# Reversed queries with one 24 KB bias table, and query and gate writes issued by ScalarE, in a hybrid decoder block

## The chip, the cores and the metric

The kernel runs on one core of one Trainium2 chip. The metric is device time in microseconds (us), lower is better; a time given for a kernel is the median of its runs. A profiled execution of the kernel before gives the trace from which all rows here are taken. The engines: TensorE (PE; PEld are its weight loads), VectorE (DVE), ScalarE (ACT), GpSimd (POOL) and SyncE (SP). SP and ACT also issue DMAs; their instruction queues appear as SPq and ACTq.

## The reference, cut to what matters

One decoder block over 512 tokens of width 1024, in float32. A state-space branch (S5) and a sliding-window attention run in parallel on the same normalized input, are merged by gates, projected and added to the input; a mixture of 16384 single-neuron experts (PEER) follows. The part that is changed is attention, with its queries, its relative-position bias and the gates' way to memory:

```python
q = rms_norm(q.reshape(bsz, seq, N_KV_HEADS, Q_PER_KV, HEAD_DIM), q_norm_g)   # 16 heads of 64
scores = jnp.einsum('bnqkgd,bnskd->bnkgqs', qb, kb).astype(jnp.float32) * scale   # blocks of 128 queries, 256 keys
dist = ATTN_BLOCK + qi - si
band_ok = (dist >= 0) & (dist < WINDOW)
bias = rel_bias_table.astype(jnp.float32)[t5_bucket(jnp.maximum(dist, 0))]
scores = jnp.where(valid, scores + bias, NEG_INF)
m = jnp.maximum(jnp.max(scores, axis=-1, keepdims=True), sink)
p = jnp.exp(scores - m)
p = p / (jnp.sum(p, axis=-1, keepdims=True) + jnp.exp(sink - m))
out = jnp.einsum('bnkgqs,bnskd->bnqkgd', p.astype(vb.dtype), vb)
gates = jax.nn.sigmoid(gate_logits + b_gate[layer])
```

The bias of a head depends on the distance of query and key alone. So all of it, for 128 queries and 256 keys, is a table of 384 numbers for each head, read at a shifted place for each query.

## The kernel before, in words

Large products are made to full precision by splitting both sides into a rounded part and a rest (`hi`, `lo`; `split`, L84 to L90) and adding three products (`mm3`, L92 to L96). A weight unit of 128x1024 numbers is loaded by SyncE into `raw` (three buffers, L117), rounded to `hi` by ScalarE (L124) and its rest `lo` made by VectorE, or now and then by GpSimd (L125).

Stages, in order. `front` projects keys and values (`proj_kv`), queries (`proj_q`), the state-space input (`proj_u`) and 16 gate tiles (`proj_gates`). Into the first three is woven `s5_params`, a long chain of small operations on VectorE and GpSimd (powers, rotations `sqr` and `sqi`, tables `co` and `si`, products `kps` on TensorE). `s5_mix` runs beside the first gates. Then attention: `kv_prep`, then for each of 4 blocks of queries `attn_q` (queries are loaded from memory and transposed, `qtr`, L597), for each of 16 units `attn_scores` (L620 products, L621 norm and bias, softmax) and `attn_pv` (probabilities transposed, `ptr`, L645, then the product with the values, `pvo`), with the products of `glu`, `s5_branch` and `attn_branch` as filling. The end of attention lies near 415 us; the PEER stage takes the rest of the time.

How the changed parts work before:

- `proj_q` (L541): for each of 2 halves of the heads and 4 blocks of tokens, ScalarE evacuates the product twice, as `qt` (L549, two buffers under the tag e1) and squared as `sq` (L550); VectorE sums the squares into `ssq` (L551); SyncE writes `qt` to memory, `q_d` (L553), 256 KB each. After the last, VectorE and ScalarE make the reciprocal norms `rq` (L556, L557).
- `proj_gates` (L559): VectorE multiplies (L567), ScalarE takes Tanh (L568), SyncE writes the tile to `g_d` (L569), 256 KB each, 16 times. SyncE executes in order, so weight loads behind such a write are issued after it.
- `bias_table` (L655): one small product gives `rb_m`, 16 heads x 384 numbers. ScalarE's queue writes it 128 times into `bias_d` (L668), 3 MB, so that a load with a step of 383 numbers from partition to partition (L669) finds each query's row shifted by one the other way. The load `bias` (L833), 2 MB, is issued before attention.

The order on each engine is not written by hand in this part: a scheduler sets it from the order of the program and its own estimate of times. So a change of one operation can move others.

Of the kernel before, what the change touches and what calls it, by code (L numbers as in the profile page):

```python
# [10 lines left out]
F32 = mybir.dt.float32  # L11
# [5 lines left out]
ALU = mybir.AluOpType  # L17
# [4 lines left out]
NT = T // 128  # L22
KD = D // 128
EPS = 1e-6
# [3 lines left out]
def r32(ap):  # L28
    return ap.bitcast(F32)
# [29 lines left out]
class Builder:  # L59
# [481 lines left out]
    def proj_q(self, xh, xl, ssq, qd, pool):  # L541
        nc = self.nc
        ep = self.ep
        for g in range(2):
            def ev_q(j, ps, g=g):
                qt = ep.tile([128, 512], F32, tag="e1", name=self.nm("qt"))
                sq = ep.tile([128, 512], F32, tag="e2", name=self.nm("sq"), bufs=1)
                r = self.rx[:, j:j + 1]
                nc.scalar.activation(qt, ps, AF.Copy, scale=r)  # L549
                nc.scalar.activation(sq, ps, AF.Square, scale=r)  # L550
                nc.vector.tensor_reduce(ssq[:, j, 8 * g:8 * g + 8], sq.rearrange("p (h d) -> p h d", d=64),  # L551
                                        axis=AX.X, op=ALU.add)
                nc.sync.dma_start(out=qd[j, :, 512 * g:512 * g + 512], in_=qt)  # L553
            yield from self.proj_tok(xh, xl, 512 + 512 * g, ev_q)
        rms = pool.tile([128, NT * 16], F32, name="rms")
        nc.vector.tensor_scalar(rms, ssq.rearrange("p a b -> p (a b)"), 1.0 / 64, EPS, op0=ALU.mult, op1=ALU.add)  # L556
        self.rq = self.rsqrt(pool, rms, NT * 16).rearrange("p (a b) -> p a b", b=16)  # L557

    def proj_gates(self, xh, xl, bg, gd):  # L559
        nc = self.nc  # L560
        for m in range(16):
            wh, wl = self.unit_cols(self.i["w_in"], 2048 + m * 128, 128)
            ps = self.gpsum[0].tile([128, T], F32, tag=self.gpsum[1], name=self.nm("gps"))
            for k in range(KD):
                self.mm3(ps, wh[:, k, :], wl[:, k, :], xh[:, k, :], xl[:, k, :], k == 0, k == KD - 1)
            g = self.ep.tile([128, T], F32, tag="e1", name=self.nm("gt"))
            nc.vector.tensor_mul(g, ps, self.rb)  # L567
            nc.scalar.activation(g, g, AF.Tanh, bias=bg[:, m:m + 1], scale=0.5)  # L568
            nc.sync.dma_start(out=gd[m], in_=g)  # L569
            yield 5.2  # L570

    def kv_prep(self, kv, kH, kL, vH, vL, gk):
# [15 lines left out]
    def attn_q(self, pool, n, qd, gq):  # L588
        nc = self.nc
        q = pool.tile([128, D], F32, tag="a_q", name=self.nm("a_q"), bufs=1)  # L590
        nc.sync.dma_start(out=q, in_=qd[n])
        qs = pool.tile([128, 16, 128], F32R, tag="a_qs", name=self.nm("a_qs"))
        for g in range(2):
            ps = self.ptr.tile([128, 4, 128], F32, tag="tr", name=self.nm("qtr"))
            for i in range(4):
                c = (4 * g + i) * 128
                nc.tensor.transpose(ps[:, i, :], q[:, c:c + 128], self.ident)  # L597
            for par in range(2):
                src = slice(64 * par, 64 * par + 64)
                oth = slice(64 - 64 * par, 128 - 64 * par)  # L600
                hs = slice(8 * g + par, 8 * g + 8, 2)
                nc.scalar.activation(qs[src, hs, :], ps[src], AF.Copy, scale=gq[src, :])
                nc.vector.scalar_tensor_tensor(qs[oth, hs, :], ps[src], gq[src, :], r32(qs[src, hs, :]),
                                               op0=ALU.mult, op1=ALU.subtract)
        return qs
# [30 lines left out]
    def attn_pv(self, pool, n, kvh, sc, vH, vL, aH, aL, psum):  # L636
        nc = self.nc
        nk = 1 if n == 0 else 2
        fl = lambda a: a.rearrange("p a b -> p (a b)")
        po = psum[0].tile([128, 4, 128], F32, tag=psum[1], name=self.nm("pvo"))  # L640
        half, v = divmod(kvh, 2)
        for kk in range(nk):
            ps = self.ptr.tile([128, 4, 128], F32, tag="tr", name=self.nm("ptr"))
            for i in range(4):
                nc.tensor.transpose(ps[:, i, :], sc[:, i, kk * 128:kk * 128 + 128], self.ident)  # L645
            ph = pool.tile([128, 4, 128], F32R, tag="a_ph", name=self.nm("a_ph"))
            pl = pool.tile([128, 4, 128], F32R, tag="a_pl", name=self.nm("a_pl"))
            self.split(ph, pl, ps)
            kt = n if n == 0 else n - 1 + kk
            vs = slice(128 * half, 128 * half + 128)  # L650
            self.mm3(fl(po), vH[:, kt, vs], vL[:, kt, vs], fl(ph), fl(pl), kk == 0, kk == nk - 1)
        rows = slice(64 * v, 64 * v + 64)
        a = (rows, slice(4 * half, 4 * half + 4), slice(n * 128, n * 128 + 128))
        self.split(aH[a], aL[a], po[rows])

    def bias_table(self, pool, dp):
        nc, I = self.nc, self.i
        tab = pool.tile([32, 16], F32, name="rb_t")
        oh = pool.tile([32, 384], F32, name="rb_o")
        mk = pool.tile([16, 384], F32, name="rb_m")  # L660
        nc.scalar.dma_start(out=tab, in_=I["rel_bias"])
        nc.scalar.dma_start(out=oh, in_=I["bucket_onehot"])
        nc.scalar.dma_start(out=mk, in_=I["band_mask"])
        ps = self.ptr.tile([16, 384], F32, tag="tr", name="rb_p")
        nc.tensor.matmul(ps, tab, oh, start=True, stop=True)
        nc.vector.tensor_add(mk, mk, ps)
        bd = dp.tile([16, 128, 384], F32, name="bias_d")
        nc.scalar.dma_start(out=bd, in_=mk[:, None, :].to_broadcast([16, 128, 384]))  # L668
        return bass.AP(tensor=bd.tensor, offset=bd.offset + 127, ap=[[383, 128], [128 * 384, 16], [1, 256]])  # L669

    def glu(self, pool, yg, zH, zL):
        nc = self.nc
# [729 lines left out]
    def consts(self, pool):  # L1402
        nc = self.nc
        self.ident = pool.tile([128, 128], F32, name="ident")
        make_identity(nc, self.ident)
        first = pool.tile([128, 1], F32, name="first")
        nc.vector.memset(first, 0.0)
        nc.scalar.activation(first, first, AF.Square)
        self.iota16 = pool.tile([128, 128, 8], F16, name="iota16")
        nc.gpsimd.iota(self.iota16, pattern=[[1, 128], [0, 8]], base=0, channel_multiplier=0, allow_small_or_imprecise_dtypes=True)  # L1410
# [67 lines left out]
```

## Time and profile before

| What | Value |
|---|---|
| Median of 3 runs | 1686.6 us (1686.0 to 1687.74) |
| Profiled execution, own time | 1682.35 us |
| Its span in the trace | 1680.6 us |
| TensorE busy | 1612.1 us, 96% of the span |
| VectorE busy | 1423.3 us, 85% |
| ScalarE busy | 840.6 us, 50% |
| GpSimd busy | 528.5 us, 31% |
| Written to memory, read from memory | 56.23 MB, 375.66 MB |

The span is what the profiler sees of the execution; 1.75 us lie around it. The share of busy time is a mean over stages with different limits: a stage's own limit is read from a table of windows, and an engine's gap from the row behind it, which names in brackets how long the engine was idle and what released it.

### The profile page before, as it was taken

To read this page: it belongs to the slowest core of one execution; us is meant where nothing else is said; L and a number is where in the kernel's file an instruction comes from. 1 tells how busy PE (TensorE), PEld (TensorE's weight loads), DVE (VectorE), ACT (ScalarE), POOL (GpSimd) and SP (SyncE) were. 2 spreads that over 40 slices of the span, in tenths; PEclk is the share of its full clock that TensorE was granted. 3 is DMA by queue.
4 is the path that set the end of the run, shared out by engine and by line. 5 is a ranking of instruction groups with operands and counts; after the bars stand their busy time and mean duration, and the time that the engine had idled before them with its cause. 6 is when DMAs were issued, how large, how long until landed. Compare 5 with 4: busy or idle time off the path is not lost.

```text
span 1680.6 us, 25288 instructions
## 1 busy us (share of the span) xinstructions
PE 1612.1 (96%) x8831; PEld 1420.8 (85%) x8831; DVE 1423.3 (85%) x2931; ACT 840.6 (50%) x1290; POOL 528.5 (31%) x472
## 2 busy tenths in 40 slices
PE   7789999998999999999999999999999999999998
PEld 5577887786899999989998999888888888888887
DVE  7699868897798899999998975887787887887885
ACT  5256566565565346665776873333333333333332
POOL 2564022332631422222332323332332332332330
PEclk9899999999999999999999999999999999999999
DMA  7823353645764667877886999999999999999993
GB/s 233 156 91 91 113 185 94 195 139 168 219 188 153 227 245 260 290 276 262 285 287 245 330 332 365 324 324 337 336 355 338 335 347 351 328 342 361 360 309 146
DMA packets 239184, 433.56 MB, mean 258 GB/s; under 512 B 17696, under 2 KB 155984, under 8 KB 235984
## 3 DMA queue, kind: packets, MB, share of 16 engines
q1 hardware_dynamic: 175904, 242.69, 43.1%
q0 software_dynamic: 36864, 134.23, 22.6%
q10 hardware_dynamic: 26288, 55.02, 10.2%
q8 instruction: 69, 1.13, 0.3%
q14 instruction: 59, 0.48, 0.1%
HBM read 375.66 MB, written 56.23 MB: 257 GB/s over the span
## 4 chain that ended last, share of the span: by engine, by line
PE 68%; DVE 11%; issue 3%; ACT 2%; DMA 2%; POOL 0%; SPq 0%; DVEq 0%; ACTq 0%; POOLq 0%
PE po L1162 11%; PE po L1161 11%; PE po L1164 11%; PE pa L94 9%; PE pa L96 9%; PE pa L95 8%; DVE lo L125 3%; PE pg L1092 1%; PE pg L1093 1%; DVE sp_row L1211 1%; DVE t_s L966 1%; DVE t_ix L968 1%; DMA raw<-w_ab 1%; DVE t_ix L972 1%; DMA gl<-g_d 1%
## 5 line engine op out<-in xcount | busy, mean ns | idle before, releaser
L124 ACT CAST hi<-t_raw 128x1024 fp32r<-128x1024 f32 x256 | 269.3, 1052 | 229.4 <-PE pa L95 138.2
L125 DVE TENSOR_TENSOR lo<-t_raw,hi 128x1024 fp32r<-128x1024 f32 x256 | 313.4, 1224 | 78.6 <-ACT hi L124 71.2
L94 PE MATMUL pa<-x2h,hi 128*128 128x384 f32 x1024 | 346.9, 339 | 11.2 <-ACT u_g L1136 11.2
L96 PE MATMUL pa<-x2h,lo 128*128 128x384 f32 x1024 | 347.6, 340 | 1.7 <-DVE lo L125 1.7
L95 PE MATMUL pa<-x2l,hi 128*128 128x384 f32 x1024 | 344.9, 337 | 0.0
L1194 POOL DMA_INDIRECT sp_row<-peer_u,sp_ei x128 | 174.3, 1362 | 385.2 <-DVE sp_row L1211 342.6
L1194 POOL DMA_INDIRECT sp_row<-peer_v,sp_ei x128 | 168.5, 1317 | 394.2 <-DVE sp_acc L1213 365.8
L1162 PE MATMUL po<-lo,v_wh 128*128 128x512 f32 x768 | 266.5, 394 | 0.0
L1161 PE MATMUL po<-hi,v_wh 128*128 128x512 f32 x768 | 242.3, 394 | 0.0
L1164 PE MATMUL po<-hi,v_wl 128*128 128x512 f32 x768 | 241.0, 394 | 0.0
L94 PEld LDWEIGHTS pa<-x2h,hi 128*128 128x128 f32 x1024 | 193.5, 189 | 15.6 <-ACT u_g L1136 13.6
L1151 ACT CAST v_wh<-v_w 128x384 fp32r<-128x384 f32 x128 | 65.6, 513 | 275.0 <-DVE v_w L1150 169.1
L96 PEld LDWEIGHTS pa<-x2h,lo 128*128 128x128 f32 x1024 | 193.5, 189 | 4.3 <-DVE lo L125 3.9
L95 PEld LDWEIGHTS pa<-x2l,hi 128*128 128x128 f32 x1024 | 193.4, 189 | 0.9
L1164 PEld LDWEIGHTS po<-hi,v_wl 128*128 128x128 f32 x768 | 143.7, 187 | 35.6
L1162 PEld LDWEIGHTS po<-lo,v_wh 128*128 128x128 f32 x768 | 143.6, 187 | 34.6
L1161 PEld LDWEIGHTS po<-hi,v_wh 128*128 128x128 f32 x768 | 143.5, 187 | 34.0
L1213 DVE SCALAR_TENSOR_TENSOR sp_acc<-sp_row,sp_a,sp_acc 128x1024 f32<-128x1024 f32 x128 | 163.8, 1280 | 0.3
L1211 DVE SCALAR_TENSOR_TENSOR sp_row<-sp_row,xrow 128x1024 f32<-128x1024 f32 x128 | 156.1, 1219 | 4.5 <-DMA sp_row<-peer_u,sp_ei 4.5
L124 ACT CAST hi<-raw 128x1024 fp32r<-128x1024 f32 x88 | 91.9, 1047 | 88.5 <-PE gps L95 15.5
L125 POOL TENSOR_TENSOR lo<-raw,hi 128x1024 fp32r<-128x1024 f32 x28 | 70.3, 2509 | 116.4 <-ACT hi L124 104.6
L1108 ACT COPY g_one<-g_o 128x1024 f16<-128x1024 f16 x48 | 99.1, 2065 | 6.4 <-ACT u_g L1136 2.4
(455 smaller groups left out, 2977.6 us busy)
## 6 DMA issues: line engine op xcount, KB each, us to landing
t_raw<-peer_uT SPq DMA_DIRECT2D x128, 512.0 KB
t_raw<-peer_v SPq DMA_DIRECT2D x128, 512.0 KB
G_d<-g_st ACTq DMA_DIRECT2D x24, 1024.0 KB
v_g<-G_d SPq DMA_DIRECT2D x64, 384.0 KB
raw<-w_in SPq DMA_DIRECT2D x32, 512.0 KB
A_d<-u_g ACTq DMA_DIRECT2D x78, 192.0 KB
v_a<-A_d SPq DMA_DIRECT2D x78, 192.0 KB
raw<-w_ab SPq DMA_DIRECT2D x64, 128.0 KB
```

The lines of the kernel that those rows point to most:

```text
L94: mm(out, lh, rh, start=first, stop=False)
L95: mm(out, lh, rl, start=False, stop=False)
L96: mm(out, ll, rh, start=False, stop=last)
L124: self.nc.scalar.copy(hi, raw)
L125: (self.nc.gpsimd if pool_lo else self.nc.vector).tensor_sub(lo, raw, r32(hi))
L1108: nc.scalar.copy(one, o1.rearrange("p b t -> p t b"))
L1161: mm(po[j][i], wh[:, c], hi[:, hs[i]], start=first, stop=False)
L1162: mm(po[j][i], wh[:, c], lo[:, hs[i]], start=False, stop=False)
L1164: mm(po[j][i], wl[:, c], hi[:, hs[i]], start=False, stop=last)
L1194: nc.gpsimd.indirect_dma_start(out=got[k], out_offset=None, in_=self.i[n], in_offset=bass.IndirectOffsetOnAxis(ap=ei[:, s:s + 1], axis=0))
L1211: nc.vector.scalar_tensor_tensor(r, r, 1.0, xrow, op0=ALU.mult, op1=ALU.mult, accum_out=av[:, s:s + 1])
L1213: nc.vector.scalar_tensor_tensor(acc, r, av[:, s:s + 1], acc, op0=ALU.mult, op1=ALU.add)
```

## The change

Attention's queries are taken in reversed order within their block. A matrix `flip`, ones on the other diagonal, is built at the start, and the product with it takes the place of the transpose in `attn_q`: it transposes the queries and reverses them. With query 127 in partition 0, each partition's row of the bias table begins one number further on than the one before, so a single copy of the table can be read with a step of one number: `bias_d` has 16x384 numbers, 24 KB, in place of 128 copies. Before the product with the values the probabilities are turned back by the same product (`attn_pv`). The reciprocal norms are reversed once, by a product with `flip` and a copy. Scores, softmax and values are computed as before. Besides, the writes of `q_d` and `g_d` are issued by ScalarE.

```diff
                 nc.scalar.activation(sq, ps, AF.Square, scale=r)
...
-                nc.sync.dma_start(out=qd[j, :, 512 * g:512 * g + 512], in_=qt)
+                nc.scalar.dma_start(out=qd[j, :, 512 * g:512 * g + 512], in_=qt)
             yield from self.proj_tok(xh, xl, 512 + 512 * g, ev_q)
-        rms = pool.tile([128, NT * 16], F32, name="rms")
-        nc.vector.tensor_scalar(rms, ssq.rearrange("p a b -> p (a b)"), 1.0 / 64, EPS, op0=ALU.mult, op1=ALU.add)
-        self.rq = self.rsqrt(pool, rms, NT * 16).rearrange("p (a b) -> p a b", b=16)
+        rms = ssq.rearrange("p a b -> p (a b)")
+        nc.vector.tensor_scalar(rms, rms, 1.0 / 64, EPS, op0=ALU.mult, op1=ALU.add)
+        rq = self.rsqrt(pool, rms, NT * 16)
+        ps = self.ptr.tile([128, NT * 16], F32, tag="tr", name="rq_ps")
+        nc.tensor.matmul(ps, self.flip, rq, start=True, stop=True)
+        nc.scalar.copy(rms, ps)
+        self.rq = ssq
...
-            nc.sync.dma_start(out=gd[m], in_=g)
+            nc.scalar.dma_start(out=gd[m], in_=g)
...
-                nc.tensor.transpose(ps[:, i, :], q[:, c:c + 128], self.ident)
+                nc.tensor.matmul(ps[:, i, :], q[:, c:c + 128], self.flip, start=True, stop=True)
...
-                nc.tensor.transpose(ps[:, i, :], sc[:, i, kk * 128:kk * 128 + 128], self.ident)
+                nc.tensor.matmul(ps[:, i, :], sc[:, i, kk * 128:kk * 128 + 128], self.flip, start=True, stop=True)
...
-        bd = dp.tile([16, 128, 384], F32, name="bias_d")
-        nc.scalar.dma_start(out=bd, in_=mk[:, None, :].to_broadcast([16, 128, 384]))
-        return bass.AP(tensor=bd.tensor, offset=bd.offset + 127, ap=[[383, 128], [128 * 384, 16], [1, 256]])
+        bd = dp.tile([16, 384], F32, name="bias_d")
+        nc.scalar.dma_start(out=bd, in_=mk)
+        return bass.AP(tensor=bd.tensor, offset=bd.offset, ap=[[1, 128], [384, 16], [1, 256]])
...
+        self.flip = pool.tile([128, 128], F32, name="flip")
+        nc.gpsimd.memset(self.flip, 0.0)
+        nc.gpsimd.affine_select(out=self.flip, in_=self.flip, compare_op=ALU.not_equal, fill=1.0, base=-127,
+                                pattern=[[1, 128]], channel_multiplier=1)
```

The change also moves instructions. Three places follow, each as the engine's row stands before and then as it stands now; the numbers behind names only tell buffers apart, and lines of the changed kernel are up to 4 higher.

SyncE's queue during the query projection, before: writes of queries (`q_d`) stand between weight loads (`raw`).

```order
L117 DMA raw_1446<-w_in 128x2x512
L553 DMA q_d<-qt_1106 128x512
L117 DMA raw_1511<-w_in 128x8x128
L553 DMA q_d<-qt_1118 128x512
L553 DMA q_d<-qt_1130 128x512
L117 DMA raw_1560<-w_in 128x8x128
L553 DMA q_d<-qt_1142 128x512
L117 DMA raw_1609<-w_in 128x8x128
```

The same queue now:

```order
L117 DMA raw_1451<-w_in 128x2x512
L117 DMA raw_1518<-w_in 128x8x128
L117 DMA raw_1567<-w_in 128x8x128
L117 DMA raw_1616<-w_in 128x8x128
L117 DMA raw_1665<-w_in 128x8x128
```

The writes are gone from between the loads; the same holds further down for the 16 writes of gates.

ScalarE's row in the same place, before: the bias write is issued some rows ahead; the first three blocks of queries are evacuated as `qt` and `sq`.

```order
L668 DMA bias_d<-rb_m 2048x1x384
L103 ACTIVATE rs_s_698<-k_ss 128x16
L124 CAST hi_1096<-raw_1094 128x1024
L124 CAST hi_1242<-raw_1240 128x1024
L103 ACTIVATE rs_s_468<-m_81_461 128x16
L124 CAST hi_1272<-raw_1270 128x1024
L549 ACTIVATE qt_1106<-tps_708,rx 128x512
L550 ACTIVATE sq_1107<-tps_708,rx 128x512
L549 ACTIVATE qt_1118<-tps_709,rx 128x512
L550 ACTIVATE sq_1119<-tps_709,rx 128x512
L549 ACTIVATE qt_1130<-tps_710,rx 128x512
```

ScalarE's row now:

```order
L672 DMA bias_d<-rb_m 16x384
L103 ACTIVATE rs_s_703<-k_ss 128x16
L124 CAST hi_1101<-raw_1099 128x1024
L124 CAST hi_1247<-raw_1245 128x1024
L103 ACTIVATE rs_s_473<-m_81_466 128x16
L124 CAST hi_1277<-raw_1275 128x1024
L549 ACTIVATE qt_1111<-tps_713,rx 128x512
L550 ACTIVATE sq_1112<-tps_713,rx 128x512
L553 DMA q_d<-qt_1111 128x512
L549 ACTIVATE qt_1123<-tps_714,rx 128x512
L553 DMA q_d<-qt_1123 128x512
L550 ACTIVATE sq_1124<-tps_714,rx 128x512
```

The bias write keeps its place and shrinks; each write of queries stands behind the activation that makes its tile.

TensorE's row where the first probabilities are transposed (`ptr`), with the second block of queries (`qtr`) and score products (`scp`) about them, before:

```order
L645 MATMUL ptr_2792<-ident,a_sc_2331 128x128 x4
L597 MATMUL qtr_2848<-ident,a_q_2845 128x128 x2
L620 MATMUL scp_2392<-kH,a_qs_2312 128x256
L620 MATMUL scp_2392<-kL,a_qs_2312 128x256
L620 MATMUL scp_2399<-kH,a_qs_2312 128x256
L620 MATMUL scp_2399<-kL,a_qs_2312 128x256
L597 MATMUL qtr_2848<-ident,a_q_2845 128x128 x2
```

The same place now:

```order
L649 MATMUL ptr_2799<-flip,a_sc_2338 128x128
L624 MATMUL scp_2399<-kH,a_qs_2319 128x256
L624 MATMUL scp_2399<-kL,a_qs_2319 128x256
L624 MATMUL scp_2406<-kH,a_qs_2319 128x256
L624 MATMUL scp_2406<-kL,a_qs_2319 128x256
L649 MATMUL ptr_2799<-flip,a_sc_2338 128x128 x3
L601 MATMUL qtr_2855<-flip,a_q_2852 128x128 x4
```

The products with `flip` take the transposes' places, one for one, and the scheduler groups them and the products about them anew; such moves run through the whole of attention.

## Rows read from the trace of the kernel before

**Rows 1.** Windows: stretch, length, busy TensorE, weight loads, VectorE, ScalarE, GpSimd; clock; DMA.
```profile
60.00:80.00 20.00, 8.26 (x26) 5.95 (x26) 9.48 (x24) 7.38 (x14) 17.19 (x38) 0.73 0.87 177
80.00:108.00 28.00, 28.00 (x133) 23.16 (x133) 27.27 (x128) 14.46 (x25) 14.41 (x35) 0.95 0.38 113
108.00:134.00 26.00, 17.55 (x88) 14.73 (x87) 25.29 (x64) 15.97 (x33) 19.26 (x28) 0.87 0.16 50
...
150.00:205.00 55.00, 55.00 (x313) 47.76 (x312) 53.21 (x95) 29.13 (x66) 3.14 (x9) 1.00 0.37 110
...
250.00:325.00 75.00, 70.85 (x360) 57.89 (x359) 62.79 (x123) 44.27 (x110) 23.92 (x13) 1.00 0.42 126
325.00:385.00 60.00, 54.72 (x369) 48.38 (x370) 58.34 (x114) 38.45 (x93) 18.52 (x9) 1.00 0.56 164
385.00:415.00 30.00, 25.03 (x109) 17.86 (x107) 19.57 (x27) 14.09 (x27) 5.35 (x3) 0.94 0.58 158
```

**Rows 2.** DMA, 38 to 80 us: queue with packets, MB, share; then an issue.
```profile
q10 hardware_dynamic: 2064, 3.15, 65.7%
...
bias_d<-rb_m ACTq DMA_DIRECT2D x1, 3072.0 KB
```

**Rows 3.** Waits, 50 to 85 us: who for what, total us, times, longest.
```profile
ACT qt L549 <- DMA q_d<-qt: 11.4, 1, 11.4
...
ACT hi L124 <- DMA raw<-w_in: 6.3, 1, 6.3
```

**Rows 4.** Timeline of TensorE: start, length, instruction, idle before and its releaser.
```profile
62.79 0.80 PE L94 MATMUL tps<-hi,xh 128*128 128x512 f32 x1 [3.13 <-ACT sq L550]
...
78.94 1.90 PE L94 MATMUL tps<-hi,xh 128*128 128x512 f32 x3 [8.95 <-ACT hi L124]
```

**Rows 5.** Timeline of VectorE: its two gaps, and one multiply twice.
```profile
61.61 1.23 DVE L125 TENSOR_TENSOR lo<-raw,hi 128x1024 fp32r<-128x1024 f32 x1 [2.88 <-ACT hi L124]
...
67.24 0.54 DVE L283 TENSOR_TENSOR cm<-a1r,bb_im 128x128 f32<-128x128 f32 x1
...
78.92 1.23 DVE L125 TENSOR_TENSOR lo<-raw,hi 128x1024 fp32r<-128x1024 f32 x1 [8.85 <-ACT hi L124]
...
80.64 0.28 DVE L283 TENSOR_TENSOR cm<-a2r,bb_im 128x128 f32<-128x128 f32 x1
```

**Rows 6.** Timeline of GpSimd: its wait for the rotations.
```profile
91.16 0.25 POOL L281 TENSOR_TENSOR cm<-co,sqr 128x16 f32<-128x16 f32 x1 [12.72 <-DVE sqi L336]
```

**Rows 7.** Lines L553 and L569: issues, ns least/median/most, first and last.
```profile
L553 SPq DMA_DIRECT2D q_d<-qt x8: 319/339/4722, 62.2 to 107.4; - x8
...
L569 SPq DMA_DIRECT2D g_d<-gt x16: 320/338/339, 152.6 to 255.4; - x16
```

**Rows 8.** Lines L597 and L645: transposes, ns least/median/most, first and last.
```profile
L597 PE MATMUL qtr<-ident,a_q x32: 270/272/328, 221.0 to 342.3; 128*128 128x128 f32 x32
...
L645 PE MATMUL ptr<-ident,a_sc x112: 270/272/421, 253.1 to 411.2; 128*128 128x128 f32 x112
```

**Rows 9.** Timeline of TensorE: two groups of four transposes, two plain products.
```profile
88.40 0.60 PE L417 MATMUL wtr<-ident,w_re 128*128 128x128 f32 x4
88.84 0.60 PE L417 MATMUL wtr<-ident,w_im 128*128 128x128 f32 x4
...
93.94 0.38 PE L426 MATMUL kps<-f_re,wrep 128*128 128x128 f32 x2
94.16 0.39 PE L426 MATMUL kps<-f_im,wrep 128*128 128x128 f32 x2
```

**Rows 10.** Timelines: the bias load and its first use; a load of one line.
```profile
209.60 0.39 ACTq L833 DMA_DIRECT2D bias<-bias_d  x1
...
229.60 0.60 DVE L621 SCALAR_TENSOR_TENSOR a_sc<-scp,rs_y,bias 128x128 f32<-128x128 f32 x2
...
414.96 0.43 SPq L1255 DMA_DIRECT2D xrow<-g2row  x1
...
419.81 2.42 POOL L125 TENSOR_TENSOR lo<-raw,hi 128x1024 fp32r<-128x1024 f32 x1 [2.46 <-DMA xrow<-g2row]
```

## The prediction

> **What bounds the kernel now.** I read the page's busy line first, then a table of windows, then the waits and the DMA view of the window with the most idle time, and at last single rows for prices. TensorE is busy nearly the whole span (the table above), so the question is where it is not. The change ends with the attention stage (about 415 us); behind that every engine keeps its order but for one copy that trades places, so what the front wins or loses moves the end by as much.
>
> The windows [rows 1] show three kinds of stretch. From 60 to 80 us everything but GpSimd stands still: TensorE 8.26 of 20, VectorE 9.48. From 80 to 205 us VectorE is the pacemaker (27.27 of 28, 25.29 of 26, 53.21 of 55), while TensorE has 8.45 us idle between 108 and 134. From 250 us on, the attention stage, TensorE is nearly full (70.85 of 75); in 325 to 385 VectorE is fuller (58.34 of 60, TensorE 54.72); from 385 to 415 neither is (25.03 and 19.57 of 30), and chains of waits set the pace.
>
> Why the hole at 60 us? Queue 10, ScalarE's, takes 65.7% of all 16 DMA engines between 38 and 80 us to move 3.15 MB [rows 2]; the only large transfer there is the write of `bias_d`. Beside it the evacuation `qt` waits 11.4 us for a write of queries, and the cast `hi` 6.3 us for a weight load [rows 3]. TensorE pays with gaps of 3.13 and 8.95 us [rows 4], VectorE with 2.88 and 8.85 us [rows 5].
>
> **The change part by part.** *The bias write shrinks from 3 MB to 24 KB.* That removes the transfer behind both gaps. Upper bound, if TensorE kept its own pace: 3.13 + 8.95 = 12.1 us of gaps, and the low clock around them. At a mean granted clock of 0.73 the 8.26 us busy in 60 to 80 hold 8.26 x 0.27 = 2.2 us of slowness, the 28 us at 0.95 hold 1.4 us [rows 1]; together 15.7 us. But VectorE stands next in line: it is full on both sides of the hole, so it sets what is won. It was idle 2.88 + 8.85 = 11.7 us. During some 10 us of these GpSimd was computing (17.19 of 20 us in the window) [rows 1], and VectorE is slower beside GpSimd: the same multiply takes 0.54 us at 67 us, with GpSimd busy, and 0.28 us at 80.6 us, alone [rows 5]. For the block around it I count a factor of about 1.55 (some operations slow, some not), so 10 us beside GpSimd do 6.5 us of work, and 3.5 us of the hole come back. I take 11.7 - 3.5 = **8.2 us won**. Were every operation slowed by 0.54/0.28 = 1.9, 4.8 us would come back and 6.9 us be won. GpSimd itself has room: it waits 12.72 us for VectorE before 91.16 us [rows 6], more than it loses.
>
> *Queries and gates are written by ScalarE.* The 8 + 16 issues take 0.34 us each [rows 7] and now stand in ScalarE's row behind the activation whose result they send, which is ScalarE's own. That is 2.7 us before 110 us, where ScalarE is half idle (14.46 of 28), and 5.4 us between 150 and 255 us, where it is busy 29.13 of 55 [rows 1] and its casts run ahead of TensorE. Queued behind each issue are the next `qt`, `sq` or `hi`; for them TensorE waits only at group changes. I take 0, at worst the 2.7 us on VectorE's and TensorE's path (the gain is then 4.2). For SyncE the queue is cleared: weight loads no longer stand behind a Tanh. Between 150 and 205 us TensorE is busy all 55 us, so nothing is won by that there. Were SyncE's weight loads in truth held by those writes and not by the volume of the bias write, the gain would be the same, since both go.
>
> *The transposes become products.* 32 transposes of queries and 112 of probabilities [rows 8] are now plain fp32 products with `flip`. A transpose of 128x128 costs TensorE 0.44 / 4 = 0.11 us (four from 88.40 to 88.84); a plain fp32 product of that size stands as two records and costs 0.22 us (93.94 to 94.16) [rows 9]. So 144 x 0.113 = **16.3 us** of work is added to TensorE. Of it 8 products fall near 220 us and 60 (44 + 16) in 250 to 325, where TensorE is full: 68 x 0.113 = 7.7 us, paid. 52 (44 + 8) fall in 325 to 385: 5.9 us, beside 5.28 us of TensorE idle under a full VectorE; I take half the idle time as cover, 2.6 us. 24 fall in 385 to 415: 2.7 us; the products stand in the waited-for chain from scores to the value product, so I count them whole. Cost 16.3 - 2.6 = 13.7 us. Far bounds: with all idle time of 250 to 415 us used (4.15 + 5.28 + 4.97 = 14.4) it would be 1.9 us, with none 16.3 us.
>
> The trace tells of two records for each plain fp32 product, hence twice the transpose. The Trainium skill, page "FP8 and Floating Point Precision", section "TensorE Precision Notes", speaks of four passes for true FP32; if that meant four times the 0.11 us, this part would cost 144 x 0.33 = 47.5 us. No row here shows that price; the 128x128 product says otherwise.
>
> *The bias load reads one 24 KB table.* 2 MB as before in pieces of 1 KB, but all from the same few lines of DRAM. It is issued at 209.60 us and first used at 229.60 us [rows 10], 20 us later. The nearest row of a load that reads one short line for all partitions is `xrow`: 512 KB, issued at 414.96, waited for until 419.81 at the latest [rows 10], so at most 4.9 us; four times that is 19.4 us, still in time. Cost 0, upper end 2 us. *The rest:* the reciprocal norms are turned by one product of 64 columns and one small copy, some 0.3 us about 80 us ahead of their use; `flip` is built on an idle GpSimd at the start. 0.
>
> **Sum.** -8.2 + 13.7 = +5.5 us. The profiled execution took 1682.35 us (span 1680.6), so 1687.9 us on its scale. The three runs have their median at 1686.6, which is 4.25 us above it; on that scale 1686.6 + 5.5 = **1692 us**. Measurement tells 0.2%, that is 3.4 us, from no change.
>
> **The rivals.** *Attention has room for the products* (the other side: faster). The order of that stage is made anew with the products in it: probabilities are turned in groups of up to 8 where groups of 4 stood, further from the value products that wait for them. If this uses more than 8.1 us of the 14.4 us idle, the kernel gets faster. With a cost of 16.3 - 12 = 4.3 us: 1686.6 - 8.2 + 4.3 = 1683 us; with all of it used 1680. For it speaks that TensorE waits there in many small pieces; against, that the pieces are waits for ScalarE and VectorE, which do not become shorter. Chance 0.22.
> *The front gives little back:* VectorE and ScalarE in turn are late, gain 4.2, and the products are paid in full: +12.1 us, 1699. For it speaks VectorE at 97% from 80 us on and the new order, which puts more of the state-space chain ahead of some `lo`. Chance 0.15.
> *TensorE sets the front's pace after all:* the whole 15.7 us are won: 1686.6 - 15.7 + 13.7 = 1685, no difference. Against it speaks VectorE's 27.27 of 28. Chance 0.09.
> *The change does not do what it says:* the gaps at 60 and 70 us stay, because SyncE's loads were late for another reason: +13.7 us, 1700. Against it speaks the 65.7%. Chance 0.03. *Four passes:* 1686.6 - 8.2 + 47.5 - 2.6 = 1723 us. Chance 0.01.
>
> **How the numbers follow.** My forecast, 1692, has a chance of 0.50; its own range is 1687 to 1697 (cover in 325 to 385 between none and all, gain 6.9 to 11.7). Of that 0.13 lies within 3.4 us of before. Of the faster rival 0.04 lies within. So: faster 0.18 + 0.02 (from the third rival's edge) = 0.20; same 0.13 + 0.04 + 0.07 = 0.24; slower 0.37 + 0.15 + 0.03 + 0.01 = 0.56. The range reaches from the faster rival's middle, less its half, 1681, to the second rival, 1699.
>
> **What would show each step.** In the trace of after: the gaps at 60 and 70 us gone, and queue 10 nearly silent before 200 us; VectorE without a hole between 58 and 80 us, and the first gate's Tanh 6 to 10 us earlier. The products: 288 records where 144 stood, and 250 to 415 us longer by 11 to 14 us when measured from the first score product to the last value product. ScalarE with 24 more issues and no new wait of TensorE for it. Wrong I would be if TensorE's idle time in attention shrank by 10 us or more, or if the first Tanh came more than 12 us earlier.

## The result, and the profile after

The changed kernel takes 1696.8 us (median of 5 runs, 1696.4 to 1697.5) against 1686.6 us before: 10.2 us more between the medians, 1.0064 times as long over all runs (95% interval 1.0052 to 1.0075). The forecast was +5.5 us. The sign and the range held; the size came out nearly twice as large.

The profiled execution of the kernel before was a quick one (1682.35 us, below all its other runs). A second profile of the same kernel, taken with the experiments, has a span of 1684.5 us and is used where stages are compared below. At the marks of the table below its front agrees with the first within 0.5 us; of the other 4 us some 2 lie in attention and 2 in PEER.

The stretches of [rows 1], after the change (TensorE, weight loads, VectorE, ScalarE, GpSimd, clock, DMA share, GB/s; four of the windows):

```profile
60.00:80.00 20.00, 15.96 (x67) 11.59 (x66) 19.73 (x63) 8.61 (x15) 16.92 (x36) 0.97 0.26 80
80.00:108.00 28.00, 26.03 (x123) 21.56 (x122) 27.27 (x104) 13.48 (x25) 20.19 (x42) 0.90 0.37 113
108.00:134.00 26.00, 19.30 (x88) 15.13 (x88) 24.76 (x58) 17.82 (x39) 22.01 (x34) 0.93 0.14 41
134.00:150.00 16.00, 13.21 (x69) 11.87 (x70) 13.32 (x27) 9.49 (x18) 3.13 (x5) 0.89 0.32 90
```

The hole at 60 us is gone: VectorE is busy 19.73 of 20 us where it was 9.48, and the DMA share fell from 0.87 to 0.26. But TensorE is not full behind it. It has idle time in every stretch from 60 to 150 us and runs below full clock there.

VectorE's timeline at the second gap of [rows 5], after: the cast `lo` that stood behind 8.85 us of idle time follows at once. The multiply `cm<-a2r,bb_im` now runs beside GpSimd and takes 0.48 us, where it took 0.28 alone at 80.64 us [rows 5].

```profile
67.76 1.21 DVE L125 TENSOR_TENSOR lo<-raw,hi 128x1024 fp32r<-128x1024 f32 x1
68.89 0.48 DVE L283 TENSOR_TENSOR cm<-a2r,bb_im 128x128 f32<-128x128 f32 x1
```

TensorE's timeline of the changed kernel, its idle times between 98 and 137 us (those over 1 us):

```profile
98.31 0.49 PE L426 MATMUL kps<-f_re,wrep 128*128 128x128 f32 x2 [1.90 <-DVE tt L432]
...
120.10 1.12 PE L417 MATMUL wtr<-ident,w_re 128*128 128x128 f32 x4 [3.33 <-DVE tt L432]
...
136.79 0.80 PE L426 MATMUL kps<-f_re,wrep 128*128 128x128 f32 x2 [4.36 <-DVE tt L432]
```

The last of them is the one that matters. For 4.36 us TensorE has nothing that its order lets go ahead, and `tt`, an addition of VectorE that frees the bank for `kps`, came late. Before, TensorE waited in this way one group of `kps` earlier (5.18 us in the first profile, 3.55 in the second) and only 0.16 and 0.81 us at this last one.

The products, as tile views of `qtr` and `ptr` (before: [rows 8]): twice the records for the queries, 64 where 32 stood, and 224 where 112.

```profile
L601 PE MATMUL qtr<-flip,a_q x64: 271/275/377, 217.6 to 350.0; 128*128 128x128 f32 x64
...
L649 PE MATMUL ptr<-flip,a_sc x224: 270/275/422, 251.1 to 423.3; 128*128 128x128 f32 x112
```

### The profile page after: what moved, and what is told of

The parts are those of the page before. It is cut to its first block, busy times and chain, and to the rows that moved or that the text cites. A ratio compares the mean times of both kernels' runs of the same rounds, so it can differ in the third digit from the quotient of the medians.

```text
span 1694.9 us, 25568 instructions
## 1 busy us (share of the span) xinstructions
PE 1631.3 (96%) x8977; PEld 1444.2 (85%) x8977; DVE 1427.0 (84%) x2931; ACT 841.6 (50%) x1291; POOL 528.9 (31%) x474
## 4 chain that ended last, share of the span: by engine, by line
PE 74%; DVE 13%; ACT 5%; DMA 4%; issue 3%; SPq 0%; POOL 0%; ACTq 0%; DVEq 0%; POOLq 0%
PE po L1166 11%; PE po L1165 11%; PE po L1168 11%; PE pa L94 9%; PE pa L96 9%; PE pa L95 9%; DVE lo L125 3%; PE gps L95 1%; PE gps L96 1%; PE pg L1096 1%; PE gps L94 1%; ACT hi L124 1%; PE pg L1097 1%; PE ptr L649 1%; DMA raw<-w_ab 1%
## 5 line engine op out<-in xcount | busy, mean ns | idle before, releaser
L1155 ACT CAST v_wh<-v_w 128x384 fp32r<-128x384 f32 x128 | 65.7, 513 | 283.4 <-DVE v_w L1154 190.1
```

## The experiments

In these sets of runs the kernel before has medians of 1686.2 to 1687.0 us. To follow a gain or a loss through the program, three instructions of TensorE serve as marks: the first product `eps` (the state-space chain is done, the front ends), the last `gps` (the last gate; the first queries are turned in this stretch) and the last `pvo` (attention ends). The starts are in us, from the tile views of each kernel's trace. They are those of one profiled execution, whose own time lies up to 2.6 us to either side of the kernel's median (in the first profile of before 4.3 us below it), so the marks of two kernels compare no better than that.

| Kernel | Median | First `eps` | Last `gps` | Last `pvo` | Span |
|---|---|---|---|---|---|
| before (first profile) | 1686.6 | 147.9 | 252.9 | 414.2 | 1680.6 |
| before (second profile) | 1686.9 | 147.4 | 252.7 | 415.9 | 1684.5 |
| gates' writes moved | 1686.9 | 147.4 | 252.7 | 415.7 | 1684.6 |
| every second query write moved | 1685.1 | 148.0 | 253.0 | 416.0 | 1685.2 |
| queries' writes moved | 1691.4 | 151.7 | 257.0 | 421.3 | 1687.6 |
| both writes moved | 1691.4 | 151.8 | 256.9 | 420.0 | 1687.4 |
| the change without moved writes | 1694.9 | 140.8 | 247.3 | 424.1 | 1693.5 |
| **the change** | 1696.8 | 144.3 | 250.9 | 426.1 | 1694.9 |
| the change, transposes back | 1683.8 | 144.2 | 249.2 | 413.7 | 1682.2 |
| the change, 3 MB write back | 1707.9 | 152.5 | 258.9 | 435.3 | 1704.4 |
| 16 copies, loads on SyncE | 1688.5 | 140.5 | 256.6 | 420.0 | 1689.4 |
| 32 copies, loads on ScalarE | 1678.3 | 140.4 | 244.6 | 407.4 | 1674.8 |
| no moved writes, only queries by product | 1688.7 | 140.9 | 247.6 | 416.5 | 1684.4 |

**Both writes moved, nothing else.** Before, with the two lines of the change that name the issuing engine:

```diff
-                nc.sync.dma_start(out=qd[j, :, 512 * g:512 * g + 512], in_=qt)
+                nc.scalar.dma_start(out=qd[j, :, 512 * g:512 * g + 512], in_=qt)
...
-            nc.sync.dma_start(out=gd[m], in_=g)
+            nc.scalar.dma_start(out=gd[m], in_=g)
```

> Before, with only the 24 writes of queries and gates moved from SyncE to ScalarE; the 3 MB bias write and the transposes stay. Theory A (the 3 MB write's volume makes the hole at 60 us, the queue move is worth nothing): 1686 to 1688 us, first `kps` product within 1.5 us of before's 93.9 us, and the gaps at 62 and 79 us still there. Rival B1 (SyncE's loads are held by the writes that stand ahead of them): the hole shrinks, 1682 to 1684 us. Rival B2 (the order that the scheduler makes with the writes on ScalarE is a worse one; TensorE's gap of 4.36 us at 132 us in the changed kernel comes from it): 1689 to 1691 us.

Measured: 1691.4 us, 1.0033 times before (interval 1.0020 to 1.0046). That is nearest rival B2. The gaps of [rows 4] are still there (3.02 us before 62.27, 8.86 before 78.64) and the first `kps` starts at 94.19 us, so rival B1 falls. The first `eps` comes 4.4 us later than in the second profile of before, and from there the difference stays about the same. So this part, which the forecast put at nothing, costs.

**The change without it.** The two lines above given back to SyncE in the changed kernel.

> The changed kernel with the 24 writes given back to SyncE: the reversal and the 24 KB table alone, in before's order of the front. Theory A: 1696 to 1698 us, as the whole change. Rival B1: weight loads are held again, 1699 to 1701 us. Rival B2 (the moved writes' order costs the front 2 to 4 us): 1693 to 1695 us, and the first exponential of attention 2 to 4 us earlier than in the changed kernel (234.1 us).

Measured: 1694.9 us, again B2, and the first `eps` 3.5 us earlier than in the change (140.8 against 144.3). Against before the front is 6.6 us shorter. The first exponential starts at 230.5 us. Of the 3.5 us the median shows 1.9 (1696.8 - 1694.9), because attention takes 176.8 us here from the last `gps` to the last `pvo` and 175.2 in the change.

**Transposes back.** In the changed kernel:

```diff
-                nc.tensor.matmul(ps[:, i, :], q[:, c:c + 128], self.flip, start=True, stop=True)
+                nc.tensor.transpose(ps[:, i, :], q[:, c:c + 128], self.ident)
...
-                nc.tensor.matmul(ps[:, i, :], sc[:, i, kk * 128:kk * 128 + 128], self.flip, start=True, stop=True)
+                nc.tensor.transpose(ps[:, i, :], sc[:, i, kk * 128:kk * 128 + 128], self.ident)
```

> The changed kernel with the 144 products with the reversed matrix made transposes again (queries are then not reversed, so the biases belong to other queries): what the 24 KB table and the moved writes do without the products. Theory A (the products cost what the two traces show between the first and the last of attention, 15 us): 1681 to 1683 us. Rival C (half of it is the new order of attention, not the products themselves): 1688 to 1690 us. The forecast's own price, 13.7 us: 1683 us.

Measured: 1683.8 us, 0.9984 of before (0.9975 to 0.9992). Between the kernels with and without the 144 products lie 1696.8 - 1683.8 = 13.0 us, nearest to the forecast's 13.7. The expectation of 15 was taken against the quick first profile of before. The time that rival C gave did not come, but this run does not exclude what C says: without the products the scheduler gives attention before's order back, on TensorE, VectorE, ScalarE and GpSimd to the last instruction (issues of DMAs aside). The 13.0 us are thus the price of the products and of attention's new order together.

**The 3 MB write back.** In the changed kernel, behind the write of the 24 KB table; no other instruction changes its place on any engine:

```diff
+        big = dp.tile([16, 128, 384], F32, name="big_d")
+        nc.scalar.dma_start(out=big, in_=mk[:, None, :].to_broadcast([16, 128, 384]))
```

> The changed kernel, and beside its 24 KB table the 3 MB write again, right behind it on ScalarE's queue, to a tensor that nobody reads; every engine's order is that of the changed kernel. Theory A (the write's removal is worth what is left of the front's gain at 205 us, 3.5 us): 1700 to 1701 us. Rival D (it is worth the 8.2 us that VectorE wins up to 80 us, and the moved writes and the new order lose the rest): 1704 to 1706 us. Rival E (the hole has another cause): 1697 us.

Measured: 1707.9 us, 11.1 us above the change and above all three expectations; nearest is D. In the trace the first `eps` is 8.2 us later and the last `pvo` 9.2 us; the profiled execution was 1.6 us quicker than this kernel's median, so the trace does not show where the last of the 11.1 us lie. The timeline of TensorE in this kernel has both gaps of [rows 4] again, within 0.2 us of their old sizes and 0.4 us of their old places, and the DMA issue tells how long the write takes (last figure: us from issue to landing):

```profile
62.88 0.50 PE L94 MATMUL tps<-hi,xh 128*128 128x512 f32 x1 [3.31 <-ACT sq L550]
...
79.25 1.90 PE L94 MATMUL tps<-hi,xh 128*128 128x512 f32 x3 [8.87 <-ACT hi L124]
```

```profile
big_d<-rb_m ACTq DMA_DIRECT2D x1, 3072.0 KB, 36.5
```

So the volume of this one write makes the hole. That part of the theory stands.

**Which of the moved writes costs, and why.** Two kernels move one group of writes each, a third moves four of the eight writes of queries (`nc.scalar if j % 2 else nc.sync`). With the gates' writes alone TensorE, VectorE and GpSimd keep before's order to the last instruction. With the queries' writes alone the whole of the front's new order appears. With every second one before's order stays but for one `lo` of VectorE.

> Before, with only the 16 writes of gates moved to ScalarE. TensorE, VectorE and GpSimd keep before's order. Theory A (an issue on ScalarE delays nothing that TensorE waits for): within 1.5 us of before, 1685 to 1688 us. Rival (16 issues of 0.34 us stand in the way of the casts `hi`): up to 5.4 us more, 1691 us.

> Before, with only the 8 writes of queries moved to ScalarE. The order of the front changes exactly as with all 24 moved. Theory A (the new order is what costs: a cast `lo` now stands ahead of the `tt` for which TensorE waits): 1689 to 1692 us, and the first `eps` product 3 to 5 us later than before's 147.9 us. Rival (the issues on ScalarE cost, most of them being those of the gates): within 1.5 us of before.

> Before, with every second write of queries (4 of the 8) moved to ScalarE. With these four the order comes out as before's on TensorE and GpSimd, and on VectorE but for one `lo`. Theory A (the cost of the moved writes is the new order, not the issues): within 1 us of before up to the first `eps` product, 1686 to 1688 us. Rival (the issues on ScalarE, or the queue that they share, cost): half of what all eight cost, 2 us, 1689 us.

Measured: 1686.9 us for the gates (0.9999, 0.9990 to 1.0008), 1691.4 us for the queries (1.0023, 1.0014 to 1.0032), 1685.1 us for every second query write (0.9989, 0.9980 to 0.9998). Theory A holds in all three (the last came out 0.9 us below its range): issues on ScalarE cost nothing that can be measured, neither sixteen nor four; the order that the scheduler makes with all eight costs some 4 us. A kernel with all eight moved and before's order kept was not run, so that the order does it rests on these three runs and on the rows that follow.

How it costs them is seen on VectorE. In the kernel with only the queries' writes moved, `lo` stands between the copies `up` and the last `tt`:

```profile
137.30 4.88 DVE L500 COPY up<-ut 32x128 f32<-32x128 f32 x8
142.21 1.65 DVE L125 TENSOR_TENSOR lo<-raw,hi 128x1024 fp32r<-128x1024 f32 x1
143.89 0.30 DVE L432 TENSOR_TENSOR tt<-kps,di 32x128 f32<-32x128 f32 x1
```

With every second write moved it stands ahead of `up`, as before, and `tt` ends 1.3 us sooner:

```profile
135.55 1.22 DVE L125 TENSOR_TENSOR lo<-raw,hi 128x1024 fp32r<-128x1024 f32 x1
136.80 0.28 DVE L432 TENSOR_TENSOR tt<-kps,di 32x128 f32<-32x128 f32 x1
137.11 4.79 DVE L500 COPY up<-ut 32x128 f32<-32x128 f32 x8
...
142.55 0.30 DVE L432 TENSOR_TENSOR tt<-kps,di 32x128 f32<-32x128 f32 x1 [0.32 <-ACT tt L434]
```

TensorE pays for it three times. Its timeline with the queries' writes moved, around the `kps` that waits for that `tt`:

```profile
144.24 0.51 PE L426 MATMUL kps<-f_re,wrep 128*128 128x128 f32 x2 [4.38 <-DVE tt L432]
144.57 0.61 PE L426 MATMUL kps<-f_im,wrep 128*128 128x128 f32 x2
...
147.39 0.75 PE L95 MATMUL gps<-xl,hi 128*128 128x512 f32 x1
...
151.68 0.50 PE L449 MATMUL eps<-up,el 128*128 128x128 f32 x3
```

The same place in the second profile of before:

```profile
142.29 0.49 PE L426 MATMUL kps<-f_re,wrep 128*128 128x128 f32 x2 [0.81 <-DVE tt L432]
142.61 0.39 PE L426 MATMUL kps<-f_im,wrep 128*128 128x128 f32 x2
...
144.09 0.47 PE L95 MATMUL gps<-xl,hi 128*128 128x512 f32 x1
...
147.39 0.83 PE L449 MATMUL eps<-up,el 128*128 128x128 f32 x6
```

The window of those eight pairs of `kps` records, in the kernel with the queries' writes moved (the last three numbers: granted clock, DMA share, GB/s):

```profile
144.24:147.39 3.15, 3.15 (x16) 3.15 (x17) 2.99 (x10) 2.00 (x5) 0.20 (x1) 0.55 0.57 167
```

`kps` starts 1.95 us later. After 4.38 us without work TensorE runs the eight pairs in 3.15 us instead of 1.80, at a granted clock of 0.55, near the lower of its two levels (1.2 instead of 2.4 GHz); in the second profile of before it is 1.00 there. That is 1.35 us. And only 7 gate products stood ahead of the wait, where before 10 did; 17 instead of 14 stand between `kps` and `eps`, at 0.23 us each, and the first of them still runs at the low clock (0.58 us to the next, for 0.32). So `eps` begins 4.29 instead of 3.30 us after the first of them: 1.0 us. Together 4.3 us, which is the whole delay of the first `eps` (151.68 against 147.39).

**A short write without the reversal.** If the volume is the cause, fewer copies in memory do as well as none. With 16 copies each of eight loads serves 16 partitions; the loads were given to SyncE, which leaves the order of the other engines as before:

```diff
-        bd = dp.tile([16, 128, 384], F32, name="bias_d")
-        nc.scalar.dma_start(out=bd, in_=mk[:, None, :].to_broadcast([16, 128, 384]))
-        return bass.AP(tensor=bd.tensor, offset=bd.offset + 127, ap=[[383, 128], [128 * 384, 16], [1, 256]])
+        bd = dp.tile([16, 16, 384], F32, name="bias_d")
+        nc.scalar.dma_start(out=bd, in_=mk[:, None, :].to_broadcast([16, 16, 384]))
+        return [bass.AP(tensor=bd.tensor, offset=bd.offset + 127 - 16 * g, ap=[[383, 16], [16 * 384, 16], [1, 256]])
+                for g in range(8)]
...
-        nc.scalar.dma_start(out=bias, in_=bias_src)
+        for g, src in enumerate(bias_src):
+            nc.sync.dma_start(out=bias[16 * g:16 * g + 16], in_=src)
```

> Before, with 16 copies of the bias table instead of 128: a write of 384 KB instead of 3 MB, and eight loads of 16 partitions on SyncE's queue in place of one on ScalarE's; TensorE, VectorE and GpSimd keep before's order to the last instruction. It prices the volume of the write alone. Theory A (worth what the products' kernel without the moved writes showed at 181 us against before's 188, some 7 us, and nothing of it is given back later): 1678 to 1681 us. Rival (the attention stage gives part of it back, as in the kernel with transposes in the changed order): 1682 to 1684 us.

Measured: 1688.5 us, no gain (1.0006, 0.9996 to 1.0015). Both expectations missed. The front is right, the first `eps` at 140.5 us. The gain is lost at one place and right behind it, TensorE's first product of the queries:

```profile
222.60 1.09 PE L597 MATMUL qtr<-ident,a_q 128*128 128x128 f32 x4 [8.54 <-issue]
```

Behind the wait, from 222 to 231 us, TensorE's granted clock is 0.63; that makes some 3 us more (8.40 us busy x 0.37). SyncE's own queue shows where the wait comes from: the load of the first queries, `a_q`, stands behind the eight loads of the table (start, time of the issues, how many):

```profile
199.45 5.22 SPq L835 DMA_DIRECT2D bias<-bias_d  x8
206.51 0.34 SPq L591 DMA_DIRECT2D a_q<-q_d  x1
```

The DMA view of 199 to 223 us has the times to landing: 15.9 us for that `a_q`, where the median over the four loads of queries is 5.2 us in the same kernel.

```profile
bias<-bias_d SPq DMA_DIRECT2D x8, 256.0 KB, 13.4
...
a_q<-q_d SPq DMA_DIRECT2D x1, 512.0 KB, 15.9
```

**The same with the loads on ScalarE.** 32 copies, four loads of 32 partitions, issued by ScalarE as the single load was (the diff above with 32 for 16, 4 for 8, `nc.scalar` for `nc.sync`).

> Before, with 32 copies of the bias table: a write of 768 KB and four loads of 32 partitions, both on ScalarE's queue, so that no load stands ahead of the queries on SyncE's. Theory A (the write's volume costs 7 us; with 16 copies they were lost again only because the queries waited behind the eight loads): the first `eps` product at 140.5 to 142 us, the first score product at 221 to 223 us, 1679 to 1682 us in all. Rival (every shorter write only moves the wait, attention takes the gain back): 1685 to 1688 us.

Measured: 1678.3 us, 0.9952 of before (0.9939 to 0.9966), faster than both kernels and a little better than expected. The first `eps` is at 140.4 us and the gain is still there at the last `pvo` (407.4 against 415.9). Its profiled execution was 1.8 us quicker than its median. TensorE no longer waits for the queries: `a_q` is issued at 199.00 us, now ahead of the table's loads, which follow from 202.09 us on ScalarE's queue. The order of the engines is before's but for one gate tile near 221 us. The write takes 9.9 us to land:

```profile
bias_d<-rb_m ACTq DMA_DIRECT2D x1, 768.0 KB, 9.9
```

**Only the queries by product.** The change without moved writes, with the 112 products of `attn_pv` made transposes again and the 32 of `attn_q` kept.

> The changed kernel with its writes given back to SyncE, and the 112 products of the probabilities made transposes again (the outputs' queries then stand in reversed order); the 32 products of the queries stay. Theory A (about 0.1 us for each product, wherever TensorE is full): 32 products cost 3 to 4 us, and with the write's 7 us won the time is 1682 to 1684 us. Rival (the cost lies in the chain from scores to the value product, so the 112 cost all of it): 1679 to 1681 us.

Measured: 1688.7 us, 4.7 us above theory A's range and 7.7 above the rival's; both fall in this form. From the last `gps` to the last `pvo` it takes 168.9 us against 163.2 before, though only 24 of the products lie there; counted by their number they would cost 2.7 us. The other 112 then cost 176.8 - 168.9 = 7.9 us (the change without moved writes has 176.8 us in this stretch), where their number would make 12.7. The medians say it more strongly: 1688.7 is 10.4 us above the 1678.3 of the kernel with 32 copies, which has no products, and the other 112 products add only 6.2 (1694.9 - 1688.7), where their number would make 3.6 and 12.7. How the sum divides is thus not a matter of counting. The order of attention was made anew in this kernel too. Where attention has before's order, as in the change with its transposes back, the stretch takes from 161.3 to 164.5 us over the kernels of the table, so 5.7 us are more than that scatter. What of them is order and what is the product was not separated.

## Why the prediction was partly right

**The cause of the hole: right.** The 3 MB write alone brings both gaps back, and a 768 KB write without any reversal removes them. SyncE's writes standing between the loads were not the cause: with all of them moved and the 3 MB kept, the front is no shorter.

**The gain in the front, 8.2 us with bounds 4.2 and 15.7: right in mechanism, and near in size.** VectorE is ahead by 80.64 - 68.89 = 11.75 us on a multiply just behind the hole, and then loses about 3.4 us because operations that ran alone now run beside GpSimd (0.48 for 0.28 us): at the addition that makes `bb_re` for the second half, 87.08 us before and 78.73 us after, 8.35 us are left, where the forecast had 8.2. The change has another order here; in the kernel with 32 copies the same operations in before's order take 9.97 us (69.06 to 79.03) instead of 6.44 (80.64 to 87.08), which is the forecast's 3.5 us. At the first `eps` in before's own order 6.6 to 7.0 us remain (140.8 and 140.4 against 147.4). In the medians the short write alone is worth 8.7 us (1678.3 against 1687.0 in the same set of runs). VectorE, not TensorE, set what was won, as the forecast chose: the bound of 15.7 was far off.

**The moved writes, 0: the step that failed.** The forecast costed 24 issues of 0.34 us and the queue behind them, and that part holds: sixteen issues of the gates cost nothing. What it had not priced is that the scheduler makes another order for the front when the eight writes of queries are on ScalarE. It saw that order, and named it within the second rival as what could put the state-space chain ahead of some `lo`; but it took VectorE's work up to attention as moved without loss. One `lo` of 1.65 us ahead of a `tt` and three gate products behind a wait cost 4.3 us in before's front and 144.3 - 140.8 = 3.5 us in the changed one; in the medians it is 4.5 us (1691.4 against 1686.9) and 1.9.

**The products, 13.7 us with bounds 1.9 and 16.3: the sum near, its parts not.** 13.0 us lie between the medians with and without them when the writes are moved, 16.6 when they are not (1694.9 against the 1678.3 of the 32 copies): the forecast lies between the two. In the window from the last `gps` to the last `pvo` TensorE's busy time and clock are, in the second profile of before:

```profile
253.09:416.34 163.25, 148.20 (x820) 122.03 (x818) 139.47 (x259) 96.09 (x227) 45.38 (x22) 0.98 0.51 146
```

and in the changed kernel:

```profile
251.27:426.47 175.20, 163.26 (x956) 142.53 (x955) 141.19 (x259) 97.01 (x227) 48.03 (x22) 0.96 0.46 136
```

Busy time grows by 15.1 us for the 136 products that lie here (136 x 0.113 = 15.4 by the forecast's price), and idle time falls from 15.05 to 11.94, by 3.1 us; the forecast had 2.6 us of cover. With the first eight products, in the stretch of the gates, it is some 1.3 us more. The mean clock is lower, 0.96 for 0.98; that is part of the 15.1. So in this pair of traces the added time is work and lower clock and not new waits, which fits the forecast's price. But the kernel with the queries' products alone shows that the cost does not follow their number stage by stage, as the forecast counted it, and attention's new order was never taken apart from the products. That the sum came out so near is in part luck.

**The load from one 24 KB table, 0: right.** It lands 8.0 us after its issue at 206.1 us, 12 us ahead of its first use at 226.05 us.

**The sum.** By the marks, against the second profile of before: -3.1 us at the first `eps` (-6.6 for the write, +3.5 for the order), -1.8 at the last `gps`, +10.2 at the last `pvo`, +10.4 in the span. The medians differ by 10.2. So the forecast's 5.5 lacks the 3.5 us of the order and 1.6 us of a front gain counted too high; the products were 0.4 us less by the two profiles (1.3 + 12.0).

The medians divide it otherwise. With the short write alone (32 copies) the time is 8.7 us below before; the products then add 16.6 us and the moved writes 1.9, or the moved writes first 5.5 (to 1683.8) and the products 13.0. So products and moved writes are not independent; together they cost 18.5 us where the forecast had 13.7 and 0, and by this account the miss lies with them and not with the front (the 9.8 us in all are 0.4 short of 10.2, as the medians of before differ by that between the sets).

**The rivals.** "The front gives little back" (4.2 us, then 1699) has nearly the right price and the wrong ground: not VectorE and ScalarE late in turn, but an order, and one that puts a `lo` ahead of the chain's `tt` and not the chain ahead of a `lo`. "Attention has room" falls: it needed 8.1 us of idle time used, and 3.1 were. "TensorE sets the front's pace" falls with VectorE's 19.73 of 20 us. "The change does not do what it says" falls with the gaps.

"Four passes" was wrongly priced. Gate products of 512 columns, with both sides split into rounded parts, follow each other every 0.23 us in the changed kernel:

```profile
216.60 0.40 PE L96 MATMUL gps<-xh,lo 128*128 128x512 f32 x1
216.84 0.39 PE L94 MATMUL gps<-xh,hi 128*128 128x512 f32 x1
217.06 0.39 PE L95 MATMUL gps<-xl,hi 128*128 128x512 f32 x1
```

For 128 columns that is 0.057 us, and the plain product's 0.22 us [rows 9] is 3.9 times it. The Trainium skill, page "FP8 and Floating Point Precision", section "TensorE Precision Notes", gives true FP32 four passes, and this agrees with it; the transpose at 0.11 us already takes two such times. The prediction set the rule against the transpose, which was the wrong unit.

**What was to be seen.** The hole and its gaps are gone, queue 10 moves 1.07 MB between 38 and 80 us at 6.9%, the records doubled, and from the first score product to the last value product attention is longer by 13.1 us against the second profile of before (225.61 to 426.47 against 228.59 to 416.34): inside the 11 to 14. Against the first profile, from which the forecast was made, it is some 15 us and outside. The first Tanh came 5.1 us earlier (146.72 against 151.86 in the first profile), just outside the 6 to 10. The sign on ScalarE held in the main: the new wait of 4.36 us at 136.79 is one for VectorE, not for ScalarE. New waits for ScalarE's copies `el` are short (0.53, 0.38 and 0.97 us between 108 and 130 us); whether the issues or the new order make them was not separated.

## What to carry to other kernels

A large write early in a program costs what it holds up; before paying arithmetic to avoid it, look for a way to write less. Here a quarter of the copies and four loads gave 8.7 us, and the reversal that saved the rest of the bytes cost 13 to 17 us, most of it as work of the fullest engine.

Where a scheduler sets the order, moving a DMA to another engine's queue is a change of order first. Compare the order on the engines that wait for one another, and price the two or three places where a long operation now stands ahead of a short one that another engine waits for. And look what a moved load is now issued ahead of: eight loads put ahead of the queries took back a whole gain of some 8 us.

## What the runs showed of the hardware

A write of 3 MB from 16 partitions in rows of 1.5 KB took 36.5 us to land, and 768 KB 9.9 us: 86 and 79 GB/s, with 65.7% of all sixteen DMA engines' time held by it between 38 and 80 us in the kernel before [rows 2]. Transfers of other queues waited through it: between 38 and 80 us the weight loads on SyncE's queue took 18.5 us to land beside the 3 MB write put back into the change, and 3.8 us in the change.

```profile
raw<-w_in SPq DMA_DIRECT2D x4, 512.0 KB, 18.5
...
raw<-w_in SPq DMA_DIRECT2D x5, 512.0 KB, 3.8
```

The Trainium skill, page "DMA: Bandwidth & Descriptors", section "Issuing engines are not separate DMA queues", says that transfers issued by different engines run on the same sixteen DMA engines and interleave; the 3 MB write agrees, as it held up SyncE's loads from ScalarE's queue. The two kernels with short tables add that it matters what is issued first: 2 MB on SyncE's queue ahead of `a_q` (199.45 against 206.51 us) cost 8.5 us of TensorE's time; on ScalarE's queue, and behind `a_q` (202.09 against 199.00), none. Whether the queue or only the order in time makes the difference was not separated.

After 4.38 us without work TensorE's granted clock was 0.55, and eight short pairs of products then took 3.15 us instead of 1.80. That wait cost a third more than its own length (1.35 of 4.38 us).
